# x turned by VectorE in 32x32 blocks instead of by TensorE, in a two-layer decoder trunk on one core

## The chip, the core and the metric

The kernel runs on one core of a Trainium2 chip. The metric is the device time of one execution in microseconds. The kernel before takes 2053.56 us, the median of three runs (2053.30 to 2054.64). One more execution was taken with the hardware profiler; the traces quoted below are of that one.

The engines are named as in the profile: PE is TensorE (PEld its weight loads), DVE VectorE, ACT ScalarE, POOL GpSimd, SP the engine that issues nearly all DMAs. A line such as L155 is a line of the kernel before unless it is said to be of the changed one.

## The reference, cut to what matters

```python
x = x + concat([main, mo]) @ w_out[l]        # once for each of the two layers
# layer 0:
h = rmsnorm(x, g_mix[0])                      # x * rsqrt(mean(x*x) + EPS) * g
z = h @ w_in_a[0]                             # D = 2048 -> 3584 columns
main = spatial_gating(z[..., :G_W], z[..., G_W:2 * G_W], g_v, w_sp, b_sp)
mo = memory_attention(z[..., 2 * G_W:], mem, g_mem[0], w_mem_kv[0])
# after each mixer a gated ConvFFN; layer 1 uses multi-head latent attention
```

The input x has 256 positions and 2048 features, `mem` 256 tokens of 2048 features, all float32. Both layers' keys and values of `mem` depend on no x: `rmsnorm(mem, g_mem[l]) @ w_mem_kv[l]` (2048 to 1024 columns each).

## The kernel before, in words

All matrix products are done in pieces that TensorE takes at its fast rate: each float32 operand is split into a rounded part (hi) and the rest (lo), and three products, hi·hi, hi·lo and lo·hi, are summed. A **chunk** is one 512 KB load of weights into a tile `raw` (four buffers), split by ScalarE into `whi` (four buffers) and by VectorE into `wlo` (five), and used by 24 matmuls of 256 columns (`gemm_fm`, L152, L153, L155) or 12 of 512 columns (`gemm_tm`, L184 to L186). SP issues the load of a chunk as soon as the `raw` buffer that is due comes free, so loads, splits and products run as a pipeline, some chunks ahead of PE.

Activations are kept feature-major: `self.x` (tile `xT`) holds x transposed, 16 blocks of 128 features by 256 positions, and `self.xhl` (tile `xhl`) its halves, multiplied with the gain `g_mix` by `split_gain` (L245 on ScalarE, L246 on VectorE). The root of the mean square is applied later, to the products.

The function `start` does four stages of eight chunks each: keys of `mem` for layer 0 (`first_keys`, in a hand-written order), its values (`gemm_tm`), keys for layer 1 (`gemm_fm`) and its values (`gemm_tm`). A table `hooks` hangs extra work behind chunk n of a stage. From there a scheduler orders the instructions on each engine by its own estimate, within the order in which they were written; `keep_in_program_order` and `manual_schedule` fix some of it. In the kernel before, the hooks bring x in like this:

- `token_load` (L391) loads a quarter of x in rows of 2 KB into the token-major tile `xtok`, in the chunks 0 to 3 of the second stage.
- `token_transpose` (L395) turns two feature blocks with four 128x128 transposes each on PE (L400) into PSUM; `put_x` (L452) splits them from PSUM and copies them into `xT` with ScalarE (L455).
- `token_squares` (L406) sums the squares of x per token on ScalarE; `token_rstd` makes the root `rt` (128x2, one token per partition), and `spread` (L420) makes from it, with two PE matmuls against a diagonal tile, `rb` (root along the free axis on all partitions).
- `conv_consts` (L329) loads four rows of constants `craw` of each ffn and turns them with four PE transposes (L337).

`layer_a` follows: three groups of eight chunks by `gemm_tm` whose evictions apply a Gelu scaled by `rt` (L775), then the rest by `gemm_fm`, whose evictions use `rb`. Its hooks load the spatial weights into the tile `wsp` (four DMAs of 128-byte pieces, L761), which takes the memory of `memhl` and so must wait until PE is done with `start`; VectorE turns them in 32x32 blocks (L766) and multiplies them with a mask (L767). They also load `positions` and, with small instructions on VectorE, make the rotary angles (`rope_angles`, with one PE transpose, L352). At the end of the program the function `turn` in `run` does the opposite of the change for layer 1: it turns `xT` in 32x32 blocks (L1114) and writes them with DMAs of 128-byte pieces (L1118).

Of the kernel before, what the change touches and what calls it, by code (L numbers as in the profile page):

```python
# [8 lines left out]
F32 = mybir.dt.float32  # L9
# [3 lines left out]
AF = mybir.ActivationFunctionType  # L13
ALU = mybir.AluOpType
AX = mybir.AxisListType

P = 128
D = 2048
S = 256
NB = D // P  # L20
# [49 lines left out]
class Kernel:  # L70
# [171 lines left out]

    def split_gain(self, hl, x, g):
        nc = self.nc
        nc.scalar.activation(hl[:, :S], x, AF.Copy, scale=g)  # L245
        nc.vector.scalar_tensor_tensor(hl[:, S:], x, g, hl[:, :S].bitcast(F32), ALU.mult, ALU.subtract)  # L246


    def rstd(self, out, sums, n, pool, tag):
# [79 lines left out]
    def conv_consts(self, l):  # L329
        nc, t = self.nc, self.t  # L330
        nf = 2 * FB
        acc = self.psum()
        for j in range(4):
            cr = self.tmp(self.gp, [nf, P], "craw", 4)
            src = t["conv_w"][l, j] if j < 3 else t["conv_b"][l]
            nc.sync.dma_start(out=cr, in_=src.rearrange("(k p) -> k p", p=P))
            nc.tensor.transpose(acc[:, j * nf : (j + 1) * nf], cr, self.ident[:nf, :nf])  # L337
        nc.vector.tensor_copy(self.cT[:, l], acc[:, : 4 * nf].rearrange("p (j k) -> p j k", j=4))

# [48 lines left out]
        nc.vector.tensor_copy(self.sinT, acc[:, S:])  # L388


    def token_load(self, src, tok, k0, k1):  # L391
        c = slice(k0 * P, k1 * P)
        self.nc.sync.dma_start(out=tok[:, :, c], in_=src.rearrange("(a p) c -> p a c", p=P)[:, :, c])

    def token_transpose(self, tok, k0, k1, put):  # L395
        for k in range(k0, k1, 2):
# [23 lines left out]
    def spread(self, out, r):  # L420
        nc = self.nc
        acc = self.psum()
        for tb in range(2):
            dg = self.tmp(self.cp, [P, P], "diag", 1)
            nc.vector.tensor_scalar(dg, self.ident, r[:, tb : tb + 1], None, ALU.mult)
            nc.tensor.matmul(acc[:, tb * P : (tb + 1) * P], self.ones, dg, start=True, stop=True)
        nc.scalar.activation(out, acc[:, :S], AF.Copy)


    def start(self):  # L430
        nc, t, tc = self.nc, self.t, self.tc
# [4 lines left out]
        self.mv = [pool.tile([P, 2, MW], F32, name=self.uid("mv")) for pool in (self.mk, self.cp)]  # L436
        self.rt = self.cp.tile([P, 2], F32, name="rt0")
        self.rb = self.tmp(self.cp, [P, S], "rbc", 2)
        with tc.tile_pool(name="st", bufs=1) as st:
            self.gp = st  # L440
            mtok = st.tile([P, 2, D], F32, name="mtok")
            xtok = st.tile([P, 2, D], F32, name="xtok")
            mrt = st.tile([P, 2], F32, name="mrt")
            mrb = st.tile([P, S], F32, name="mrb")

# [3 lines left out]
                nc.scalar.activation(hi, a, AF.Copy)  # L449
                nc.vector.tensor_tensor(mhl[:, k : k + 2, S:], a, hi.bitcast(F32), ALU.subtract)  # L450

            def put_x(k, acc):  # L452
                for i in range(2):
                    self.split_gain(self.xhl[k + i], acc[:, i * S : (i + 1) * S], self.gain("g_mix", k + i))
                nc.scalar.activation(self.x[:, k : k + 2, :], acc.rearrange("p (k s) -> p k s", k=2), AF.Copy)  # L455

            mload = lambda k0, k1: lambda: self.token_load(t["mem"][0], mtok, k0, k1)
            mturn = lambda k0, k1: lambda: self.token_transpose(mtok, k0, k1, put_mem)
            xload = lambda k0, k1: lambda: self.token_load(t["x"][0], xtok, k0, k1)
            xturn = lambda k0, k1: lambda: self.token_transpose(xtok, k0, k1, put_x)  # L460
            mpart = st.tile([P, 2, 4], F32, name="mpart")
            xpart = st.tile([P, 2, 4], F32, name="xpart")
            msq = lambda j: lambda: self.token_squares(mtok, mpart, j, st)
            xsq = lambda j: lambda: self.token_squares(xtok, xpart, j, st)

            def scale_keys():
                self.spread(mrb, mrt)
# [9 lines left out]
            def first_keys(evict):  # L477
# [62 lines left out]
                for b, acc in enumerate(accs):  # L540
# [2 lines left out]
            hooks = [  # L543
                None,
                {
                    0: [lambda: self.gains(("g_mix", "g_ffn", "g_kv")), xload(0, 4), msq(0), msq(1)], 1: [xload(4, 8), msq(2), msq(3)],
                    2: [lambda: self.token_rstd(mpart, st, mrt), xload(8, 12)], 3: [xload(12, 16), xturn(0, 4)], 4: [self.masks],
                    6: [lambda: self.gains(("g_v", "g_kv_lat", "g_q_lat"))],
                },
                {0: [xturn(4, 8)], 1: [scale_keys], 2: [xturn(8, 12)], 4: [xturn(12, 16)], 6: [xsq(0)]},  # L550
                {
                    0: [xsq(1)], 1: [xsq(2)], 2: [xsq(3), lambda: self.conv_consts(0)], 3: [lambda: self.token_rstd(xpart, st, self.rt)],
                    5: [lambda: self.spread(self.rb, self.rt), lambda: self.conv_consts(1)],
                },
            ]
            for l in range(2):
# [12 lines left out]
                m = lambda k: mhl[:, k, :]  # L569
                g = lambda k: self.gain("g_mem", l * NB + k)  # L570
# [9 lines left out]
    def three(self, o, w, x, start, stop):  # L580
        mm, (wh, wl), (xh, xl) = self.nc.tensor.matmul, w, x
        mm(o, wh, xh, start=start, stop=False)  # L582
        mm(o, wh, xl, start=False, stop=False)  # L583
        mm(o, wl, xh, start=False, stop=stop)  # L584
# [149 lines left out]
                g0 += ng  # L734


    def layer_a(self):
        nc, t, tc = self.nc, self.t, self.tc
        w, xhl, rt, rb = t["w_in_a"][0], self.xhl, self.rt, self.rb
        x = lambda k: xhl[k]  # L740
        ks = list(range(NB))
        with ExitStack() as ctx:
            la = ctx.enter_context(tc.tile_pool(name="la", bufs=1))
# [19 lines left out]
            def spatial_turn(g):  # L763
                w4 = wT[:, g : g + 4, :]
                k3 = self.keep.rearrange("p (g s) -> p g s", g=1).to_broadcast([P, 4, P])
                nc.vector.transpose(out=w4, in_=spatial["raw"][:, g : g + 4, :])  # L766
                nc.vector.tensor_tensor(w4, w4, k3, ALU.mult)  # L767

            turns = {2 + i: [lambda i=i: spatial_turn(4 * i)] for i in range(3)}
            zhooks = ({2: [lambda: self.rope_angles(la)], 5: [spatial_load]}, {4: [self.rope_tables]}, turns)  # L770
            for c in range(3):

                def evz(tb, acc):
# [30 lines left out]
            hl = self.ap.tile([P, NB, 512], F32R, tag="big", name=self.uid("mainhl"))  # L804
            p, parts = {}, {}
# [388 lines left out]
```

## Time and profile before

| | |
|---|---|
| median of three runs | 2053.56 us |
| profiled execution | 2053.87 us, of which the span 2052.2 us |
| granted TensorE clock | 0.999 |
| start to about 104.3 us | the four stages of `start` |
| from about 104.3 us | `layer_a` |
| L400 on x | 32 transposes, 32.5 to 72.9 us |
| x loads | four of 512 KB, issued from 22.7 to 30.8 us |

How to read it: times are from the span's start. A row of a timeline gives the start, the time that the group took, engine, line, operation, tiles and count, and in brackets the idle time just before with what ended it. PE's matmuls are pipelined, so the end of one lies beyond the start of the next; the distance between starts is what an instruction costs, its duration is not. A row of the groups ends with busy time, mean ns of one, idle time before them. A row for one line gives durations as min/median/max in ns. A row of stretches gives, after the stretch and its length, the busy time and count of PE, PEld, DVE, ACT and POOL, then the granted clock, the DMA share and GB/s. A row of waits gives the total, the number of times and the longest.

### The profile page before, as it was taken

The numbers are of one execution on the slowest core, as the hardware profiler recorded it, in microseconds if no ns is written. First come the engines' busy times: TensorE is split into PE (matmuls) and PEld (weight loads), VectorE is DVE, ScalarE is ACT, GpSimd is POOL, SyncE is SP. The second block draws the span as 40 slices with busy tenths as digits, with TensorE's granted clock in tenths as the row PEclk, the third lists the DMA queues.
The fourth block names the chain that finished last, engine by engine and source line by source line (L and its number), as shares of the span: only waits on it lengthen the run. The fifth ranks groups of instructions, "written<-read, shape, count | busy, mean of one in ns | idle before, by whom it ended". The sixth has DMA issues, their size and how long they took to land.

```text
span 2052.2 us, 39853 instructions
## 1 busy us (share of the span) xinstructions
PE 2042.1 (100%) x16304; PEld 1975.3 (96%) x16304; DVE 1401.0 (68%) x2120; ACT 1083.3 (53%) x1581; POOL 142.1 (7%) x200
## 2 busy tenths in 40 slices
PE   9999999999999999999999999999999999999998
PEld 8989999999999999999999999999988999889996
DVE  6666766777656767557778786777755667646765
ACT  7754744555434555345545575455543555435554
POOL 0000013100000000000043141400000000000000
PEclk9999999999999999999999999999999999999999
DMA  8576555566556665566555535568655666556654
GB/s 286 188 212 185 165 195 194 188 196 195 195 196 193 192 194 194 195 195 192 198 192 180 183 116 179 184 204 223 208 187 194 197 194 195 191 193 195 197 181 154
DMA packets 228987, 394.66 MB, mean 192 GB/s; under 512 B 36990, under 2 KB 44484, under 8 KB 228676
## 3 DMA queue, kind: packets, MB, share of 16 engines
q1 hardware_dynamic: 228612, 391.58, 59.6%
q8 instruction: 127, 2.08, 0.4%
q10 hardware_dynamic: 192, 0.54, 0.1%
q14 instruction: 56, 0.46, 0.1%
HBM read 387.88 MB, written 2.10 MB: 190 GB/s over the span
## 4 chain that ended last, share of the span: by engine, by line
PE 99%; ACT 0%; DVE 0%; DMA 0%; issue 0%; ACTq 0%
PE ps L152 26%; PE ps L153 26%; PE ps L155 26%; PE ps L185 6%; PE ps L184 6%; PE ps L186 6%; PE ps L507 1%; PE ps L400 0%; PE ps L583 0%; PE ps L584 0%; PE ps L582 0%; PE ps L1003 0%; PE ps L792 0%; PE ps L1031 0%; PE ps L625 0%; DMA graw<-in_g_mem 0%
## 5 line engine op out<-in xcount | busy, mean ns | idle before, releaser
L114 DVE TENSOR_TENSOR wlo<-raw,whi 128x1024 fp32r<-128x1024 f32 x660 | 818.5, 1243 | 521.9 <-ACT whi L113 516.1
L113 ACT ACTIVATE whi<-raw 128x1024 fp32r<-128x1024 f32 x660 | 700.5, 1062 | 851.7 <-PE ps L153 616.9
L152 PE MATMUL ps<-xhl,whi 128*128 128x256 f32 x3264 | 762.7, 277 | 0.0
L153 PE MATMUL ps<-xhl,whi 128*128 128x256 f32 x3264 | 761.1, 276 | 0.0
L152 PEld LDWEIGHTS ps<-xhl,whi 128*128 128x128 f32 x3264 | 612.7, 188 | 0.3
L153 PEld LDWEIGHTS ps<-xhl,whi 128*128 128x128 f32 x3264 | 612.7, 188 | 0.3
L155 PE MATMUL ps<-xhl,wlo 128*128 128x256 f32 x3264 | 436.5, 276 | 0.0
L155 PEld LDWEIGHTS ps<-xhl,wlo 128*128 128x128 f32 x3264 | 400.3, 188 | 0.0
L152 PE MATMUL ps<-h,whi 128*128 128x256 f32 x704 | 163.6, 276 | 0.0
L153 PE MATMUL ps<-h,whi 128*128 128x256 f32 x704 | 163.6, 276 | 0.0
L185 PE MATMUL ps<-wlo,h 128*128 128x512 f32 x354 | 137.2, 388 | 0.0
L184 PE MATMUL ps<-whi,h 128*128 128x512 f32 x354 | 136.8, 388 | 0.0
L186 PE MATMUL ps<-whi,h 128*128 128x512 f32 x354 | 136.8, 388 | 0.0
L153 PEld LDWEIGHTS ps<-h,whi 128*128 128x128 f32 x704 | 131.9, 188 | 0.0
L152 PEld LDWEIGHTS ps<-h,whi 128*128 128x128 f32 x704 | 131.8, 188 | 0.0
L152 PE MATMUL ps<-mainhl,whi 128*128 128x256 f32 x512 | 119.6, 277 | 0.0
L153 PE MATMUL ps<-mainhl,whi 128*128 128x256 f32 x512 | 119.3, 276 | 0.0
L694 ACT ACTIVATE c<-a,cT 128x256 f32<-128x256 f32 x176 | 99.3, 589 | 0.4 <-DVE a L232 0.3
L153 PEld LDWEIGHTS ps<-mainhl,whi 128*128 128x128 f32 x512 | 96.0, 188 | 0.0
L152 PEld LDWEIGHTS ps<-mainhl,whi 128*128 128x128 f32 x512 | 95.9, 188 | 0.0
L155 PE MATMUL ps<-h,wlo 128*128 128x256 f32 x704 | 94.1, 276 | 0.0
L232 DVE TENSOR_TENSOR a<-ps,rbc 128x256 f32<-128x256 f32 x176 | 69.9, 418 | 24.9 <-PE ps L155 24.9
(318 smaller groups left out, 2251.2 us busy)
## 6 DMA issues: line engine op xcount, KB each, us to landing
raw<-in_w_ffn_up SPq DMA_DIRECT2D x352, 512.0 KB, 3.5
raw<-in_w_ffn_down SPq DMA_DIRECT2D x176, 512.0 KB, 4.6
raw<-in_w_out SPq DMA_DIRECT2D x64, 512.0 KB, 4.3
raw<-in_w_in_a SPq DMA_DIRECT2D x56, 512.0 KB, 3.5
raw<-in_w_mem_kv SPq DMA_DIRECT2D x31, 512.0 KB, 4.4
raw<-in_w_in_b SPq DMA_DIRECT2D x16, 512.0 KB, 3.5
raw<-in_w_kv_a SPq DMA_DIRECT2D x9, 512.0 KB, 4.0
raw<-in_w_uq SPq DMA_DIRECT2D x12, 384.0 KB, 3.3
```

The source lines that it names most:

```text
L113: nc.scalar.activation(hi[:, :n], raw[:, :n], AF.Copy)
L114: nc.vector.tensor_tensor(lo[:, :n], raw[:, :n], hi[:, :n].bitcast(F32), ALU.subtract)
L152: mm(acc[:, :S], wh, x[:, :S], start=first, stop=False)
L153: mm(acc[:, :S], wh, x[:, S:], start=False, stop=False)
L155: mm(acc[:, :S], wl, x[:, :S], start=False, stop=last)
L184: mm(acc, xh, wh, start=first, stop=False)
L185: mm(acc, xh, wl, start=False, stop=False)
L186: mm(acc, xl, wh, start=False, stop=last)
L232: self.nc.vector.tensor_tensor(out, acc[:, :S], r, ALU.mult)
L507: nc.tensor.matmul(acc[:, :S], w[:, o : o + P], x, start=k == 0 and n == 0, stop=k == NB - 1 and n == 2)
L694: nc.scalar.activation(c, a, AF.Identity, scale=w(2), bias=w(3))
```

## The change

x is loaded with its positions on partitions 0 to 31 of a quarter: portion m holds positions 32m to 32m + 31, and its four DMAs put feature columns 32q to 32q + 31 of every 128 on partitions 32q to 32q + 31, in pieces of 32 floats (128 bytes). One VectorE transpose of 32x32 blocks per portion then writes 32 columns of all 16 blocks of `xT`. The portions, four DMAs of 64 KB each, are spread over hooks of the second and third stage, the transposes come two or three chunks after the loads. The squares are taken on ScalarE from `xT` (two blocks at a time) and added up by VectorE into `xsum`; the sum over partitions is a PE matmul with `ones` in the new `x_rstd`, called in chunk 4 of `layer_a`'s first group, which replaces `token_squares`, `token_rstd` and `spread` for x. The splits with gain move to the fourth stage and read `xT`. The loads of the conv constants are kept in the written order.

```diff
-    def token_load(self, src, tok, k0, k1):
-        c = slice(k0 * P, k1 * P)
-        self.nc.sync.dma_start(out=tok[:, :, c], in_=src.rearrange("(a p) c -> p a c", p=P)[:, :, c])
+    def block_load(self, src, raw, m):
+        s = src[32 * m : 32 * (m + 1), :].rearrange("i (k q j) -> q i k j", q=4, j=32)
+        for q in range(4):
+            self.tc.keep_in_program_order(self.nc.sync.dma_start(out=raw[32 * q : 32 * (q + 1), m], in_=s[q]))
...
-            nc.sync.dma_start(out=cr, in_=src.rearrange("(k p) -> k p", p=P))
+            self.tc.keep_in_program_order(nc.sync.dma_start(out=cr, in_=src.rearrange("(k p) -> k p", p=P)))
...
-            dg = self.tmp(self.cp, [P, P], "diag", 1)
+            dg = self.tmp(self.cp, [P, P], "diag", 2)
...
-            def put_x(k, acc):
-                for i in range(2):
-                    self.split_gain(self.xhl[k + i], acc[:, i * S : (i + 1) * S], self.gain("g_mix", k + i))
-                nc.scalar.activation(self.x[:, k : k + 2, :], acc.rearrange("p (k s) -> p k s", k=2), AF.Copy)
+            def xturn(m):
+                keep(nc.vector.transpose(out=self.x[:, :, 32 * m : 32 * (m + 1)], in_=xraw[:, m]))
+
+            def xput(k):
+                sq = xsum if k == 0 else self.tmp(st, [P, 512], "junk", 2).rearrange("p (k s) -> p k s", k=2)
+                keep(nc.scalar.activation(sq, self.x[:, k : k + 2, :], AF.Square))
+                if k:
+                    keep(nc.vector.tensor_tensor(xsum, xsum, sq, ALU.add))
+                for j in (k, k + 1):
+                    for ins in self.split_gain(self.xhl[j], self.x[:, j, :], self.gain("g_mix", j)):
+                        keep(ins)
+                if k == NB - 2:
+                    nc.vector.tensor_tensor(self.ssum, xsum[:, 0], xsum[:, 1], ALU.add)
...
                 {
-                    0: [lambda: self.gains(("g_mix", "g_ffn", "g_kv")), xload(0, 4), msq(0), msq(1)], 1: [xload(4, 8), msq(2), msq(3)],
-                    2: [lambda: self.token_rstd(mpart, st, mrt), xload(8, 12)], 3: [xload(12, 16), xturn(0, 4)], 4: [self.masks],
-                    6: [lambda: self.gains(("g_v", "g_kv_lat", "g_q_lat"))],
+                    0: [lambda: self.gains(("g_mix", "g_ffn", "g_kv")), msq(0), msq(1)], 1: [msq(2), msq(3)],
+                    2: [lambda: self.token_rstd(mpart, st, mrt), xload(0)], 4: [self.masks, xload(1)], 5: [xt(0)],
+                    6: [lambda: self.gains(("g_v", "g_kv_lat", "g_q_lat")), xload(2)], 7: [scale_keys, xt(1)],
                 },
-                {0: [xturn(4, 8)], 1: [scale_keys], 2: [xturn(8, 12)], 4: [xturn(12, 16)], 6: [xsq(0)]},
                 {
-                    0: [xsq(1)], 1: [xsq(2)], 2: [xsq(3), lambda: self.conv_consts(0)], 3: [lambda: self.token_rstd(xpart, st, self.rt)],
-                    5: [lambda: self.spread(self.rb, self.rt), lambda: self.conv_consts(1)],
+                    0: [xload(3)], 1: [xload(4), xt(2)], 2: [xt(3)], 3: [xload(5), xt(4)], 4: [xload(6)], 5: [xload(7), xt(5)],
+                    6: [xt(6)], 7: [xt(7)],
+                },
+                {
+                    0: [xp(0)], 1: [xp(2)], 2: [lambda: self.conv_consts(0), xp(4)], 3: [xp(6)], 4: [xp(8)],
+                    5: [lambda: self.conv_consts(1), xp(10)], 6: [xp(12)], 7: [xp(14)],
                 },
...
+    def x_rstd(self):
+        self.rstd_bc(self.rb, self.ssum, D)
+        acc = self.psum()
+        for tb in range(2):
+            self.nc.tensor.matmul(acc[:, tb : tb + 1], self.ssum[:, tb * P : (tb + 1) * P], self.ones[:, :1], start=True, stop=True)
+        self.rstd(self.rt, acc[:, :2], D, self.cp, "rt")
...
-            zhooks = ({2: [lambda: self.rope_angles(la)], 5: [spatial_load]}, {4: [self.rope_tables]}, turns)
+            zhooks = ({2: [lambda: self.rope_angles(la)], 4: [self.x_rstd], 5: [spatial_load]}, {4: [self.rope_tables]}, turns)
```

**The order on the engines.** Three places. First PE in the third stage, between the stage's first chunk and its second, in the kernel before (`ps` are accumulators, the numbers tell tiles of one name apart):

```order
L155 MATMUL ps_687<-memhl_82,wlo_691 128x256 x2
L155 MATMUL ps_688<-memhl_82,wlo_691 128x256 x2
L400 MATMUL ps_721<-ident,xtok 128x128 x4
L400 MATMUL ps_731<-ident,xtok 128x128 x4
L152 MATMUL ps_685<-memhl_82,whi_742 128x256
```

The changed kernel has no L400 with `xtok` anywhere; its x work on PE stands in chunk 5 of `layer_a`:

```order
L352 MATMUL ps_1293<-ident,pos_f 128x2
L265 MATMUL ps_1401<-ssum_89,ones 128x256
L755 MATMUL ps_1412<-ones,ssum_89 128x1 x2
```

So eight transposes here, and 32 in all, have gone, and three matmuls have come. Second SP's loads in the second stage, before:

```order
L317 DMA graw_469<-in_g_kv 16x128
L393 DMA xtok<-in_x 128x2x512
L103 DMA raw_485<-in_w_mem_kv 128x2x512
L393 DMA xtok<-in_x 128x2x512
L103 DMA raw_514<-in_w_mem_kv 128x2x512
L393 DMA xtok<-in_x 128x2x512
```

and now:

```order
L317 DMA graw_470<-in_g_kv 16x128
L103 DMA raw_485<-in_w_mem_kv 128x2x512
L103 DMA raw_513<-in_w_mem_kv 128x2x512
L394 DMA xraw<-in_x 32x16x32 x4
L103 DMA raw_548<-in_w_mem_kv 128x2x512
L103 DMA raw_568<-in_w_mem_kv 128x2x512
L394 DMA xraw<-in_x 32x16x32 x4
```

The x loads stand two weight loads later and in groups of four; the last group stands ahead of the twelfth weight load counted from `raw_548`. Third VectorE at the start of `layer_a`, before (`wlo_1426` is chunk 5 of its first group, `wlo_1450` chunk 6):

```order
L114 TENSOR_TENSOR wlo_1408<-raw_1406,whi_1407 128x1024
L350 CAST pos_f<-pos_i 2x128
L114 TENSOR_TENSOR wlo_1426<-raw_1424,whi_1425 128x1024
L766 STREAM_TRANSPOSE slots_1255<-wsp_1443 128x512 x3
L114 TENSOR_TENSOR wlo_1450<-raw_1448,whi_1449 128x1024
```

and now:

```order
L114 TENSOR_TENSOR wlo_1385<-raw_1383,whi_1384 128x1024
L788 STREAM_TRANSPOSE slots_1232<-wsp_1443 128x512 x3
L789 TENSOR_TENSOR slots_1232<-slots_1232,keep 128x512
L114 TENSOR_TENSOR wlo_1426<-raw_1424,whi_1425 128x1024
L789 TENSOR_TENSOR slots_1232<-slots_1232,keep 128x512
L350 CAST pos_f<-pos_i 2x128
```

The transposes of `wsp` and a mask product have moved ahead of chunk 5's `wlo`, and the cast behind it. On SP the four `wsp` loads are now issued together, ahead of chunk 6's load and of `in_b_sp`, which stood between them before.

More of the change, by code (lines that the diff above doesn't have):

```diff
@@ L244, in split_gain @@
         nc = self.nc
-        nc.scalar.activation(hl[:, :S], x, AF.Copy, scale=g)
-        nc.vector.scalar_tensor_tensor(hl[:, S:], x, g, hl[:, :S].bitcast(F32), ALU.mult, ALU.subtract)
+        hi = nc.scalar.activation(hl[:, :S], x, AF.Copy, scale=g)
+        return hi, nc.vector.scalar_tensor_tensor(hl[:, S:], x, g, hl[:, :S].bitcast(F32), ALU.mult, ALU.subtract)
     def rstd(self, out, sums, n, pool, tag):
@@ L438, in start @@
         self.rb = self.tmp(self.cp, [P, S], "rbc", 2)
+        self.ssum = self.tmp(self.cp, [P, S], "ssum", 2)
         with tc.tile_pool(name="st", bufs=1) as st:
@@ L441, in start @@
             mtok = st.tile([P, 2, D], F32, name="mtok")
-            xtok = st.tile([P, 2, D], F32, name="xtok")
+            xraw = st.tile([P, 8, NB, 32], F32, name="xraw")
+            xsum = st.tile([P, 2, S], F32, name="xsum")
             mrt = st.tile([P, 2], F32, name="mrt")
@@ L450, in put_mem @@
                 nc.vector.tensor_tensor(mhl[:, k : k + 2, S:], a, hi.bitcast(F32), ALU.subtract)
-            def put_x(k, acc):
-                for i in range(2):
-                    self.split_gain(self.xhl[k + i], acc[:, i * S : (i + 1) * S], self.gain("g_mix", k + i))
-                nc.scalar.activation(self.x[:, k : k + 2, :], acc.rearrange("p (k s) -> p k s", k=2), AF.Copy)
[L457 to L460, printed above, removed]
+            keep = tc.keep_in_program_order
+            def xturn(m):
[10 more added lines that the diff above has]
+                    nc.vector.tensor_tensor(self.ssum, xsum[:, 0], xsum[:, 1], ALU.add)
+            xload = lambda m: lambda: self.block_load(t["x"][0], xraw, m)
+            xt = lambda m: lambda: xturn(m)
+            xp = lambda k: lambda: xput(k)
             mpart = st.tile([P, 2, 4], F32, name="mpart")
-            xpart = st.tile([P, 2, 4], F32, name="xpart")
             msq = lambda j: lambda: self.token_squares(mtok, mpart, j, st)
-            xsq = lambda j: lambda: self.token_squares(xtok, xpart, j, st)
             def scale_keys():
```

## The prediction

> **What bounds the kernel now.** I read the page's busy times first, then its chain, then TensorE's own waits.
>
> ```profile
> PE 2042.1 (100%) x16304; PEld 1975.3 (96%) x16304; DVE 1401.0 (68%) x2120; ACT 1083.3 (53%) x1581; POOL 142.1 (7%) x200
> ...
> PE 99%; ACT 0%; DVE 0%; DMA 0%; issue 0%; ACTq 0%
> ```
>
> The chain that ends last is TensorE from end to end. The waits view of PE has three rows in all:
>
> ```profile
> PE ps L474 <- DVE ones L283: 1.1, 1, 1.1
> PE ps L583 <- DVE pT L241: 0.4, 1, 0.4
> PE ps L325 <- DMA graw<-in_g_mem: 0.4, 1, 0.4
> ```
>
> 1.9 us of waiting in a span of 2052.2, and none of it where the change works (20 to 130 us). So time is won only by instructions taken from PE, and lost only if VectorE, ScalarE or the weight loads fall so far behind that PE begins to wait. The unit below is the chunk: one 512 KB weight load, 24 matmuls of 256 columns.
>
> **The change part by part.** *PE loses the transposes of x* (the first place shown in the part on the change). Rows of PE's timeline in the third stage, where eight transposes stand between two chunks:
>
> ```profile
> 57.98 1.07 PE L155 MATMUL ps<-memhl,wlo 128*128 128x256 f32 x8
> 58.89 1.04 PE L400 MATMUL ps<-ident,xtok 128*128 128x128 f32 x8
> 61.60 1.07 PE L155 MATMUL ps<-memhl,wlo 128*128 128x256 f32 x8
> ...
> 68.55 1.07 PE L155 MATMUL ps<-memhl,wlo 128*128 128x256 f32 x8
> 71.27 1.08 PE L155 MATMUL ps<-memhl,wlo 128*128 128x256 f32 x8
> ```
>
> From one chunk's L155 to the next is 71.27 - 68.55 = 2.72 us bare and 61.60 - 57.98 = 3.62 us with eight transposes: 0.90 us for eight, the switch to and from them included. There are 32 on x: **-3.60 us**.
>
> *PE loses `spread` of x's root* (two matmuls with `diag`):
>
> ```profile
> 97.98 0.39 PE L426 MATMUL ps<-diag,ones 128*128 128x128 f32 x2
> 98.20 0.47 PE L337 MATMUL ps<-ident,craw 88*128 88x88 f32 x4
> ...
> 102.90 0.39 PE L426 MATMUL ps<-diag,ones 128*128 128x128 f32 x2
> 103.04 0.47 PE L185 MATMUL ps<-wlo,memhl 128*128 128x512 f32 x1
> 103.35 0.40 PE L186 MATMUL ps<-whi,memhl 128*128 128x512 f32 x1
> 103.59 0.40 PE L184 MATMUL ps<-whi,memhl 128*128 128x512 f32 x1
> ```
>
> 98.20 - 97.98 = 0.22, and 103.35 - 102.90 = 0.45 less one ordinary step (103.59 - 103.35 = 0.24) = 0.21: **-0.43 us**.
>
> *PE gains `x_rstd`*: a matmul of `ones` with the 256-column sum, as L265 does in the ffn, and two with one column.
>
> ```profile
> 367.70 1.07 PE L155 MATMUL ps<-xhl,wlo 128*128 128x256 f32 x8
> 368.61 0.59 PE L265 MATMUL ps<-ssum,ones 128*128 128x256 f32 x2
> 370.88 1.07 PE L155 MATMUL ps<-xhl,wlo 128*128 128x256 f32 x8
> ```
>
> 370.88 - 367.70 = 3.18, less 2.72: **+0.46 us**. An fp32 matmul shows as two passes (x2), so the one-column ones are four passes. No row has such a shape: between nothing and four passes at the 0.11 us a 128-column fp32 pass takes above (0.90 / 8), 0.44. I take **+0.40**, near the upper end, since the 128 x 128 weights are loaded all the same. Sum on PE: -3.60 - 0.43 + 0.46 + 0.40 = **-3.2 us** (-3.6 to -3.1 with the bounds).
>
> *VectorE gains* eight block transposes of 128x512, seven additions of 128x512, one of 128x256, and the root on 256 columns. The nearest rows:
>
> ```profile
> 116.22 1.90 DVE L766 STREAM_TRANSPOSE slots<-wsp 128x512 f32<-128x512 f32 x3 [3.96 <-DMA wsp<-in_w_sp]
> 118.04 1.18 DVE L114 TENSOR_TENSOR wlo<-raw,whi 128x1024 fp32r<-128x1024 f32 x1
> 119.21 1.89 DVE L767 TENSOR_TENSOR slots<-slots,keep 128x512 f32<-128x512 f32 x3
> ...
> L246 DVE SCALAR_TENSOR_TENSOR xhl<-xT,gT,xhl x32: 830/894/961, 294.7 to 1329.9; 128x256 fp32r<-128x256 f32 x32
> L246 DVE SCALAR_TENSOR_TENSOR xhl<-ps,gT,xhl x16: 470/476/484, 41.1 to 79.0; 128x256 fp32r<-128x256 f32 x16
> L246 DVE SCALAR_TENSOR_TENSOR qhl<-ql,gT,qhl x4: 474/474/474, 1151.3 to 1153.2; 128x256 fp32r<-128x256 f32 x4
> ```
>
> A transpose is 1.90 / 3 = 0.63 us, an addition 0.63: 8 x 0.63 + 7 x 0.63 + 0.4 = 9.9 us over some 75 us. The 16 splits with gain read `xT` from SBUF instead of PSUM; that is 0.47 (the `qhl` row) to 0.89 us (the `xhl<-xT` row), so 0 to 6.7 us more; I take 0, because the long rows stand where GpSimd squares the same `xT`, and it does not here. ScalarE drops eight copies and trades squares for squares. Of that, nothing is on the chain as long as VectorE's lead lasts:
>
> ```profile
> 54.44 1.42 DVE L119 SCALAR_TENSOR_TENSOR wlo<-raw,gT,whi 128x512 fp32r<-128x512 f32 x2 [1.30 <-ACT whi L118]
> ...
> 64.65 1.12 PE L155 MATMUL ps<-memhl,wlo 128*128 128x256 f32 x8
> ```
>
> That chunk's `wlo` is ready at 55.86 and used at 64.65: 8.8 us ahead. VectorE is 65 to 75% busy here (rows below), so 9.9 us spread over 27 chunks, 0.37 of each 2.72, fits: cost 0.
>
> *The loads.* x comes in 16384 pieces of 128 bytes instead of 2 KB rows. The trace has one stretch like it, where `turn` writes x back through 16 transfers of 1024 such pieces; beside it the stretch before, weights alone, and the stretches that x will now fall in:
>
> ```profile
> 1340.00:1384.00 44.00, 44.00 (x390) 44.00 (x390) 33.21 (x53) 24.95 (x33) 0.00 (x0) 1.00 0.62 192
> 1384.00:1418.00 34.00, 34.00 (x302) 34.00 (x301) 22.13 (x29) 14.62 (x19) 0.00 (x0) 1.00 0.95 206
> ...
> 42.00:56.00 14.00, 14.00 (x63) 11.33 (x62) 10.36 (x23) 11.76 (x21) 0.00 (x0) 1.00 0.64 218
> 56.00:72.00 16.00, 16.00 (x141) 15.96 (x140) 10.76 (x19) 13.35 (x27) 3.29 (x4) 1.00 0.53 174
> ...
> xt<-xs SPq DMA_DIRECT2D x16, 128.0 KB, 6.2
> ...
> DVE wlo L114 <- ACT whi L113: 12.2, 8, 4.7
> ```
>
> (last columns: clock, DMA share, GB/s). Weights cost 16 x 0.62 / 0.192 = 52 engine-us per MB. From 1384 to 1418, 7.0 MB moved in 0.95 x 16 x 34 = 517 engine-us; 4.9 MB of weights take 253, the 2.1 MB of pieces 264: 16 ns a piece, or 16.5 us of all sixteen engines, where 2 KB rows would take 6.8. The eight portions stand among twelve weight loads (SP's order, in the part on the change), 12 x 2.72 = 32 us: at a share of 0.6 the weights take 19.2 of these, with the pieces 35.7, so the feed may fall 3.7 us behind; the lead is 8.8. In the stretch quoted VectorE did wait, up to 4.7 us for one chunk (last row), and PE was busy 34.00 of 34.00. Cost 0. Each block transpose stands behind the `wlo` of a chunk whose load was issued after its own portion, so it adds no wait of its own.
>
> The Trainium skill, "DMA: Bandwidth & Descriptors", Specifications, speaks against this part: below 512 B a transfer misses line rate, by read-modify-write. The trace agrees in kind (16.5 us against 6.8 for the same bytes). By the rule alone the first rival below would be the likelier and its time the answer; by the rows the price is paid off PE's chain, and the sum stays.
>
> *The start of layer A* is where cover is thinnest. VectorE's transposes of `wsp`, which wait for the four `w_sp` loads, now stand ahead of chunk 5's `wlo`, not chunk 6's, and the cast for PE's L352 stands behind them.
>
> ```profile
> 104.28 0.40 PE L184 MATMUL ps<-whi,xhl 128*128 128x512 f32 x1
> ...
> 104.47 1.12 SPq L761 DMA_DIRECT2D wsp<-in_w_sp  x2
> ...
> 107.60 0.39 SPq L755 DMA_DIRECT2D slots<-in_b_sp  x1
> 108.04 1.60 SPq L761 DMA_DIRECT2D wsp<-in_w_sp  x2
> ...
> SPq L761 <- PE ps L186: 0.2, 1, 0.2
> ```
>
> The loads wait for PE to leave `memhl` (last row), that is for layer A's begin, T (104.28). They landed at 116.22, T + 11.9, with `in_b_sp` (0.79 MB, 0.79 x 52 / 16 = 2.6 us) among them; now it is issued after them, so about T + 9.4. Then three transposes 1.9, one mask product 0.63, `wlo` 1.2: ready T + 13.1; PE reaches it at 5 x 2.72 + 0.46 = T + 14.1. Another product and the cast end at T + 13.9, and PE's L352 stands at T + 14.5. So 0.6 us to spare, cost 0; at worst they land as late as before, and PE loses 2.5 - 0.6 = 1.9 us. Behind that, `x_rstd` adds about 4 us on VectorE (the 256-column reciprocal alone 1.75, next row) while PE goes through chunks 7 to 12. From T + 13.1 to chunk 9's `wlo` I add 10.1 us: T + 23.2, wanted at T + 25.8.
>
> ```profile
> L257 DVE RECIPROCAL rbr<-rbr 128x256 f32<-128x256 f32 x1 | 1.8, 1754 | 0.5 <-ACT rbr L256 0.5
> ```
>
> *The constants' loads* leave the first 20 us, where no chunk waited for them: 0.
>
> The profiled execution took 2053.87 us, 1.67 outside its span; 2053.87 - 3.2 = 2050.7. The median of the runs shown is 2053.56, 0.3 lower, so the forecast is **2050.4 us**, 0.16% faster.
>
> **The rivals.** *The feed starves* (slower than before). If a piece costs much more than 16 ns when it comes from HBM, the weights behind it on the same queue are late, `raw` is empty, and the lead is used up. For: the strained row above, and SP's issue of four piece transfers. Against: PE held there. It decides from (32 + 8.8 - 19.2) us x 16 / 16384 = 21 ns a piece; at twice the 16 ns, 19.2 + 33 - 40.8 = 11.4 us are lost: 2061.8. The rule above points the same way.
>
> *`w_sp` lands late*: worked out above, 2052.3; it decides from T + 10.0.
>
> *PE gets more than the pitch says.* If a transpose really holds PE for its whole duration, 32 times that is gained:
>
> ```profile
> L400 PE MATMUL ps<-ident,xtok x32: 270/272/274, 32.6 to 72.9; 128*128 128x128 f32 x32
> ```
>
> 32 x 0.272 = 8.7 instead of 3.6: 2045.3. Against it stand the 0.90 us for eight. The Trainium skill, "TensorE: Matmul & The Clock Gate", Part 4: PE-mode transpose, puts a transpose inside a kernel at about 275 ns; this trace's duration agrees, its spacing does not.
>
> *Nothing changes*: some other wait takes the 3.2 us, most likely `rt` so late that the Gelu holds ScalarE. 2053.5.
>
> **How the numbers follow.** Forecast 0.60 (2049.8 to 2051.2 by the bounds); `w_sp` late 0.12 (to 2053); feed starves 0.18, mostly over 2057.7; more from PE 0.05; nothing 0.05. About 0.2%, 4.1 us, is what a measurement of this kernel tells from no change, so -3.2 counts as the same: faster 0.11 (0.05, and 0.06 of the forecast, should the spacing of neighbouring chunks tighten by 0.9 us in all), same 0.70, slower 0.19. The range, 2049.2 to 2055.5, takes in the forecast, late `w_sp`, no change and the mildest starving.
>
> **What would show it.** Right: PE's waits view has no new row between 20 and 130 us, chunks are 2.72 us apart throughout the third stage, and layer A begins 3.6 to 4.2 us earlier. Feed: rows of PE waiting for VectorE or ScalarE in L152 to L186 before 100 us, or `whi` waiting for `raw` by several us. `w_sp`: PE waiting at chunk 5 of layer A. What would make the forecast wrong otherwise: block transposes far over 0.63 us, or one-column matmuls over 0.1 us a pass.

## The result, and the profile after

The changed kernel takes **2049.85 us** (median of 22 runs, 2049.50 to 2051.64), the kernel before 2053.43 in as many. The ratio is 0.9983, 95% interval 0.9977 to 0.9989: 3.5 us faster, between 2.3 and 4.7 (3.6 by the medians). The forecast was 2050.4, that is 3.2 us less. Both are under the 4.1 us from which the prediction counts a change, so this is its "same", to which it gave 0.70. The profiled execution took 2050.37 us with a span of 2048.6, against 2053.87 and 2052.2.

The page's busy times and chain, and then all of PE's waits, of the changed kernel:

```profile
PE 2038.7 (100%) x16274; PEld 1972.0 (96%) x16274; DVE 1411.5 (69%) x2138; ACT 1079.5 (53%) x1565; POOL 142.5 (7%) x200
...
PE 99%; ACT 0%; DVE 0%; DMA 0%; issue 0%; ACTq 0%
```

```profile
PE ps L485 <- DVE ones L283: 1.1, 1, 1.1
PE ps L597 <- DVE pT L241: 0.4, 1, 0.4
PE ps L325 <- DMA graw<-in_g_mem: 0.3, 1, 0.3
```

PE is still the wall and its waits are the same three. VectorE has 10.5 us more to do, ScalarE 3.8 less. So the gain has to lie in PE's own instructions, and where it lies can be read from the first matmul of each stage. PE's timeline before, at the begin of the second, third and fourth stage of `start` and of the part of layer A that follows its three `gemm_tm` groups (layer A's own begin, 104.28, was shown in the prediction):

```profile
32.02 0.40 PE L184 MATMUL ps<-whi,memhl 128*128 128x512 f32 x1
...
56.15 0.28 PE L152 MATMUL ps<-memhl,whi 128*128 128x256 f32 x1
...
81.25 0.40 PE L184 MATMUL ps<-whi,memhl 128*128 128x512 f32 x1
...
170.47 0.28 PE L152 MATMUL ps<-xhl,whi 128*128 128x256 f32 x1
```

and now, with layer A's begin:

```profile
31.93 0.40 PE L184 MATMUL ps<-whi,memhl 128*128 128x512 f32 x1
...
55.51 0.37 PE L152 MATMUL ps<-memhl,whi 128*128 128x256 f32 x1
...
77.38 0.40 PE L184 MATMUL ps<-whi,memhl 128*128 128x512 f32 x1
...
99.94 0.39 PE L184 MATMUL ps<-whi,xhl 128*128 128x512 f32 x1
...
166.97 0.28 PE L152 MATMUL ps<-xhl,whi 128*128 128x256 f32 x1
```

| stretch of PE | before | after | difference |
|---|---|---|---|
| span's start to the third stage | 56.15 | 55.51 | -0.64 |
| third stage (24 of the 32 transposes stood here) | 25.10 | 21.87 | -3.23 |
| fourth stage (`spread` stood here) | 23.03 | 22.56 | -0.47 |
| layer A's three groups (`x_rstd` stands here now) | 66.19 | 67.03 | +0.84 |
| from there to the span's end | 1881.73 | 1881.63 | -0.10 |
| sum | 2052.2 | 2048.6 | -3.6 |

Of the first -0.64, the second stage makes -0.55 (24.13 us before, 23.58 now). The other 0.09, like the 0.10 at the end, stands where PE's work hasn't changed; without both, the stages that the change touches give -3.41. Layer A begins 4.34 us earlier, a little more than the 3.6 to 4.2 that the prediction named as its sign.

In the third stage each chunk now follows the last at the bare distance: 62.87 - 60.15 = 2.72 us.

```profile
60.15 0.28 PE L155 MATMUL ps<-memhl,wlo 128*128 128x256 f32 x1
...
62.87 0.39 PE L155 MATMUL ps<-memhl,wlo 128*128 128x256 f32 x2
```

The price of `x_rstd` stands in chunk 5 of layer A's first group. From PE's timeline:

```profile
114.76 0.22 PE L352 MATMUL ps<-ident,pos_f 2*128 2x2 f32 x1
114.91 0.70 PE L265 MATMUL ps<-ssum,ones 128*128 128x256 f32 x2
115.45 0.50 PE L755 MATMUL ps<-ones,ssum 128*128 128x1 f32 x4
115.81 0.48 PE L185 MATMUL ps<-wlo,xhl 128*128 128x512 f32 x1
```

The four one-column passes last from 115.45 to 115.81. On VectorE, the block transposes, and a pair of splits that read `xT` from SBUF:

```profile
L458 DVE STREAM_TRANSPOSE xT<-xraw x8: 703/704/706, 42.5 to 71.8; 128x512 f32<-128x512 f32 x8
```

```profile
73.76 0.87 DVE L246 SCALAR_TENSOR_TENSOR xhl<-xT,gT,xhl 128x256 fp32r<-128x256 f32 x2
```

So far the sum holds. What the experiments had to settle is whether the covers are as thick as the prediction made them: it costed 16384 small pieces, 9.9 us of VectorE and a late `w_sp` at nothing.

### The profile page after: what moved, and what is told of

It is laid out like the page before. It is cut to its first block, busy times and chain, and to the rows that moved or that the text cites. A ratio compares the mean times of both kernels' runs of the same rounds, so it can differ in the third digit from the quotient of the medians.

```text
span 2048.6 us, 39833 instructions
## 1 busy us (share of the span) xinstructions
PE 2038.7 (100%) x16274; PEld 1972.0 (96%) x16274; DVE 1411.5 (69%) x2138; ACT 1079.5 (53%) x1565; POOL 142.5 (7%) x200
## 4 chain that ended last, share of the span: by engine, by line
PE 99%; ACT 0%; DVE 0%; DMA 0%; issue 0%; ACTq 0%
PE ps L152 26%; PE ps L153 26%; PE ps L155 26%; PE ps L184 6%; PE ps L185 6%; PE ps L186 6%; PE ps L518 1%; PE ps L597 0%; PE ps L598 0%; PE ps L596 0%; PE ps L1025 0%; PE ps L814 0%; PE ps L401 0%; PE ps L1053 0%; PE ps L639 0%; DMA graw<-in_g_mem 0%
```

## The experiments

All are made from the changed kernel. Times are to be read against 2049.85, stages against the table above. The start of the program varies by itself: among kernels that are the same up to there, the third stage begins between 54.55 and 56.53 us in their profiles. Lengths of stages don't share this: the second stage takes 23.58 to 23.68 us in all of these.

**What a transpose costs PE.** Two kernels with 24 idle transposes:

```diff
+            def one():
+                acc = self.psum()
+                nc.tensor.transpose(acc[:, :P], mtok[:, 0, :P], self.ident)
...
+            for stage in hooks[1:]:
+                for n in range(8):
+                    stage.setdefault(n, []).append(one)
```

> The changed kernel, with 24 idle PE transposes of 128x128 put back (their result is read by nobody), one behind each chunk of the second, third and fourth stage, 18 of them with no other fp32 work beside them. Theory (a transpose costs PE its distance to the next start, 0.11 us, wherever it stands): 24 x 0.11 = +2.6 us, about 2052.5, and chunks of the third stage 2.72 + 0.11 = 2.83 us apart. Rival (a transpose alone between other matmuls holds PE for its duration of 0.27 us, and is cheap only in a run of eight): +6.5 us, about 2056.4, chunks 2.99 us apart.

Measured: 2053.45 us. The third stage takes 22.83 us, 0.96 more for eight (0.12 each); the fourth 23.54, 0.98 more. PE's timeline there:

```profile
62.11 1.07 PE L155 MATMUL ps<-memhl,wlo 128*128 128x256 f32 x8
63.02 0.27 PE L473 MATMUL ps<-ident,mtok 128*128 128x128 f32 x1
64.96 1.07 PE L155 MATMUL ps<-memhl,wlo 128*128 128x256 f32 x8
```

The lone transpose shows 0.27 us and adds 64.96 - 62.11 - 2.72 = 0.13. The second stage takes 0.94 more as well, so the three stages add 2.9. The median is 3.6 us up; the 0.7 left over lies in none of these and was not explained (in its profile the second stage began late, at 32.82). Even so it is far from the rival's +6.5.

```diff
+            def eight():
+                acc = self.psum()
+                for i in range(8):
+                    nc.tensor.transpose(acc[:, i % 4 * P : (i % 4 + 1) * P], mtok[:, 0, :P], self.ident)
...
+            for n in (1, 3, 5):
+                hooks[2][n].append(eight)
```

> The changed kernel, with the same 24 idle transposes in three runs of eight, behind chunks 1, 3 and 5 of the third stage. Theory: 3 x 0.90 = +2.7 us, about 2052.5, the same as one at a time, and the chunks with a run 3.62 us apart. Rival (272 ns each): +6.5 us.

Measured: 2052.56 us, third stage 24.57, so +2.70 for 24. Both say 0.11 to 0.13 us each; the next matmul doesn't wait out the duration of 0.27. The rival that PE gets 0.272 us back per transpose is out.

**The constants' loads.**

```diff
-            self.tc.keep_in_program_order(nc.sync.dma_start(out=cr, in_=src.rearrange("(k p) -> k p", p=P)))
+            nc.sync.dma_start(out=cr, in_=src.rearrange("(k p) -> k p", p=P))
```

> The changed kernel, with the loads of the conv constants left to the scheduler again, which puts them among the first five weight loads; nothing else differs on any engine. Theory (no chunk waits for them there): 0, layer A's first matmul stays at 99.9 us. Rival (a part of the gain comes from the emptier start): slower by up to 0.4 us, all of it before the second stage begins.

Measured: 2050.26 us (2049.48 to 2051.20); the third stage begins at 55.26, layer A at 99.68, all stages as in the table. The median is 0.4 us up, which the rival allows too, but no stage is longer and layer A begins no later. So no part of the gain is seen to come from here, and 0.4 us can't be told from the start's own variation.

**The pieces left out.**

```diff
-                keep(nc.vector.transpose(out=self.x[:, :, 32 * m : 32 * (m + 1)], in_=xraw[:, m]))
+                keep(nc.vector.transpose(out=self.x[:, :, 32 * m : 32 * (m + 1)], in_=xraw[:, 0]))
...
-            xload = lambda m: lambda: self.block_load(t["x"][0], xraw, m)
+            xload = lambda m: lambda: self.block_load(t["x"][0], xraw, 0) if m == 0 else None
```

> The changed kernel, with only the first of the eight portions of x loaded, and all eight block transposes reading that one: seven eighths of the 128-byte pieces are left out. Theory (the pieces cost lead, not time): 0 (within 0.3 us), layer A's first matmul at 99.9 us, but the lead of VectorE's halves over PE in the third stage, 3.8 to 6.3 us in the changed kernel, grows to 7 or more. Rival (the pieces hold PE up somewhere): faster by 0.5 us or more.

Measured: 2049.95 us, stages 21.86, 22.56 and 67.04: no time, as expected. The lead did grow. PE's first need of a chunk is the first half of its `whi`, which ScalarE has ready 0.73 us after it starts. Chunk 22, the last but one of the third stage, on ScalarE and PE, first in the changed kernel:

```profile
67.83 4.01 ACT L118 ACTIVATE whi<-raw,gT 128x512 fp32r<-128x512 f32 x6 [1.95 <-DMA raw<-in_w_mem_kv]
```

```profile
71.94 0.28 PE L152 MATMUL ps<-memhl,whi 128*128 128x256 f32 x1
```

and without the pieces:

```profile
62.28 1.34 ACT L118 ACTIVATE whi<-raw,gT 128x512 fp32r<-128x512 f32 x2 [1.38 <-PE ps L153]
```

```profile
71.14 0.28 PE L152 MATMUL ps<-memhl,whi 128*128 128x256 f32 x1
```

71.94 - 68.56 = **3.4 us** of lead against 71.14 - 63.01 = 8.1; the bracket tells the rest, since ScalarE waits for the load in the one and for PE in the other. Seven eighths of the pieces cost 4.7 us of lead, and no time.

The DMA engines have little left either. Their share (the last column but one) in the changed kernel is 1.00 and 0.84 where it was 0.64 and 0.53 before:

```profile
42.00:56.00 14.00, 14.00 (x66) 11.44 (x66) 9.35 (x21) 8.27 (x16) 0.00 (x0) 1.00 1.00 244
56.00:72.00 16.00, 16.00 (x143) 16.00 (x143) 11.82 (x17) 9.98 (x17) 3.63 (x4) 1.00 0.84 245
```

**More pieces.** How much more could the feed have borne? Portions are loaded once more, into `mtok`, which is free by then: behind the last one, the last two, the last four, and behind each of the last four two. The edit is that of the first; the second and third have `m >= 6` and `m >= 4` in it, the fourth loads two portions for each `m > 3`.

```diff
+            xdup = mtok.rearrange("p a (b k j) -> p (a b) k j", b=4, j=32)
+            dup = lambda m: self.block_load(t["x"][0], xdup, m) if m >= 7 else None
-            xload = lambda m: lambda: self.block_load(t["x"][0], xraw, m)
+            xload = lambda m: lambda: (self.block_load(t["x"][0], xraw, m), dup(m))
```

> The changed kernel, with one portion more (2048 pieces, 4 DMAs) behind the last, into a tile that nobody reads. In the changed kernel SP issues without a pause from 42 to 63 us, 0.64 us for each of these DMAs, and the smallest lead of VectorE's halves in the third stage is 3.75 us. Theory (SP's issue time is taken from the lead): 4 x 0.64 = 2.6 us of lead lost, about 1.2 left, time unchanged, 2049.9. Rival (time of the DMA engines): 1.8 us of lead lost, time unchanged as well.

> The changed kernel, with two portions more, one behind each of the last two. Theory (SP's issue time): 8 x 0.64 = 5.1 us against 3.75 of lead, so the third stage, 21.87 us in the changed kernel, takes 1.4 us more, and some more where the granted clock falls after PE has stood: 2051.2 to 2053. Rival (engine time): 3.6 us against 3.75, time unchanged.

> The changed kernel, with four portions more, one behind each of the last four. Theory (SP's issue time): 16 x 0.64 = 10.3 us against 3.75, so 6.5 us and some clock: 2056 to 2059. Rival (engine time): 4 x 1.8 = 7.2 less 3.75 less some free time of the engines, +2: 2052.

> The changed kernel, with 16384 more pieces of 128 bytes: behind each of the portions 4 to 7 two more portions are loaded into a tile that nobody reads. Theory of the prediction (what counts is the time of the 16 DMA engines): at about 14 ns a piece 14.3 us more; the engines have about 9% of 20 us free there, and the halves lead PE by at least 3.8 us: 14.3 - 1.8 - 3.8 = +8.7 us, about 2058.5, and PE waits for halves in the third stage. Rival (SP, which needs 0.63 us for the issue of each of the 32 DMAs, 20.2 us in all, is the limit): 20.2 - 3.8 less what SP has free, 12 us or more, 2062 or later. Third: the feed has more room than either, 0 to +3.

| portions more | time | over 2049.85 |
|---|---|---|
| 1 | 2052.92 | +3.1 |
| 2 | 2055.39 | +5.5 |
| 4 | 2060.14 | +10.3 |
| 8 | 2072.70 | +22.9 |

One portion, an eighth more pieces, already costs time; both theories said it would not. (Two of its executions took 2049.9 and 2050.0, eight 2052.0 to 2054.7.) With two and four portions the theory with SP's issue time is nearer, but too low by 2.4 and 1.1 us at its upper end, and engine time is too low by 5.5 and 8. PE's timeline around chunk 22 of the run with one portion more, and its clock in two stretches behind (the column before the last two):

```profile
73.95 0.39 PE L152 MATMUL ps<-memhl,whi 128*128 128x256 f32 x1 [2.35 <-ACT whi L118]
...
76.94 1.91 PE L155 MATMUL ps<-memhl,wlo 128*128 128x256 f32 x8
78.64 0.40 PE L152 MATMUL ps<-memhl,whi 128*128 128x256 f32 x1
```

```profile
74.00:76.00 2.00, 1.89 (x12) 1.68 (x13) 2.00 (x4) 1.98 (x4) 0.00 (x0) 0.87 0.90 346
76.00:78.00 2.00, 2.00 (x11) 2.00 (x10) 2.00 (x4) 1.27 (x3) 0.00 (x0) 0.50 0.70 208
```

PE stands 2.35 us, and 1.5 us after it has begun again it is granted half its clock for some 3 us, so that the chunk takes 78.64 - 73.95 = 4.69 us instead of 2.72. The third stage is 4.61 us longer in this execution (2054.48 us), nearly twice the wait.

Why did 3.4 us of lead not carry one portion of 2.6? SP's row of one load ahead of the last two portions, in the changed kernel, and in this one with the added portion:

```profile
54.95 1.68 SPq L103 DMA_DIRECT2D raw<-in_w_mem_kv  x1
```

```profile
54.60 3.71 SPq L103 DMA_DIRECT2D raw<-in_w_mem_kv  x1
...
64.93 2.92 SPq L394 DMA_DIRECT2D mtok<-in_x  x4
```

The added DMAs take SP 2.9 us, and this load, ahead of them, 2.0 more than in the other execution. Chunk 22's load is the first of the five that follow the last portion, in the changed kernel and then here:

```profile
63.01 7.38 SPq L103 DMA_DIRECT2D raw<-in_w_mem_kv  x5
```

```profile
67.95 7.80 SPq L103 DMA_DIRECT2D raw<-in_w_mem_kv  x5
```

It is issued 4.9 us later, and ScalarE begins on it 4.8 us behind its issue in the changed kernel and 5.2 here (67.83 and 73.18). So the load is late because SP issues it late, and hardly because it takes longer. Why the load at 54.60 held SP for 3.71 us isn't shown. I take it that such pushes come and go between executions, which agrees with the two that lost nothing; that they do in the changed kernel as well wasn't shown.

With eight portions more, a row of SP's timeline and what its eight DMAs took, two stretches of the core, and PE's largest row of waits:

```profile
60.61 7.09 SPq L394 DMA_DIRECT2D mtok<-in_x  x8
```

```profile
L394 SPq DMA_DIRECT2D mtok<-in_x x8: 581/626/2383, 60.6 to 67.1; - x8
...
DMA to landing us min/median/max: 2.4/2.5/2.7
```

```profile
56.00:72.00 16.00, 11.39 (x94) 10.66 (x92) 4.07 (x6) 2.91 (x5) 2.83 (x4) 1.00 0.82 167
72.00:88.00 16.00, 10.09 (x48) 9.50 (x48) 3.46 (x5) 2.67 (x4) 0.00 (x0) 0.68 0.76 126
```

```profile
PE ps L152 <- ACT whi L118: 14.2, 4, 5.9
```

The DMA share is 0.82 and 0.76, so the sixteen engines are not full; SP issues without a pause from 47 to 88 us (its 48 DMAs of pieces take 35.9 us of these, 0.75 each), and PE waits 14.2 us in four waits. The eight DMAs of the row land 2.4 to 2.7 us after their issue, x's in the changed kernel after 3.2 to 5.2, so these don't stand long at the engines. That bears out the rival with SP's issue time as the limit, which said 12 us or more; engine time alone (+8.7) is wrong. The Trainium skill, "Perfetto Trace Analysis", What "DMA-bound" means, names this case: an issuing sequencer that is solid with DMA slices is the bound, and what it does in them is make descriptors. The trace agrees that SP issues without a pause; what SP does meanwhile no run here shows.

The same bytes in larger pieces:

```diff
+            xrow = lambda c: tc.keep_in_program_order(
+                nc.sync.dma_start(out=mtok[:, :, c], in_=t["x"][0].rearrange("(a p) c -> p a c", p=P)[:, :, c]))
-            xload = lambda m: lambda: self.block_load(t["x"][0], xraw, m)
+            xload = lambda m: lambda: (self.block_load(t["x"][0], xraw, m), m > 3 and xrow(slice(512 * (m - 4), 512 * (m - 3))))
```

> The changed kernel, with the same 2 MB more at the same four places, in four loads of 512 KB with pieces of 2 KB, into a tile that nobody reads. Theory (engine time): 1024 pieces at about 90 ns are 5.8 us of the 16 engines, 5.8 - 1.8 - 3.8 = 0, so the time stays at 2049.9 (to +1); the distance to the run with 128-byte pieces is what the size of the pieces costs. Rival (bytes count, not pieces): the same loss as with the small pieces.

Measured: 2057.93 us, +8.1. So 2 MB cost 22.9 - 8.1 = 14.8 us more in 128-byte pieces and 32 DMAs than in 2 KB pieces and four; these runs don't separate the size of the pieces from the number of DMAs. The theory's "nothing" for the rows was wrong, and so was the rival's "the same loss". Here the engines are full, in the stretch in which PE falls behind:

```profile
56.00:72.00 16.00, 13.85 (x118) 13.25 (x117) 6.16 (x9) 6.66 (x11) 3.19 (x4) 1.00 1.04 247
72.00:88.00 16.00, 14.86 (x91) 13.65 (x92) 11.83 (x22) 10.05 (x19) 0.00 (x0) 0.89 0.88 285
```

And the eight portions issued by GpSimd, with the engine as a further argument of `block_load` (the edit is against the kernel with eight portions more):

```diff
-            dup = lambda m: [self.block_load(t["x"][0], xdup, 2 * m - 8 + i) for i in range(2 * (m > 3))]
+            dup = lambda m: [self.block_load(t["x"][0], xdup, 2 * m - 8 + i, nc.gpsimd) for i in range(2 * (m > 3))]
```

> The changed kernel, with the 16384 further pieces of the run that cost 22.9 us, but issued by GpSimd from its own queue (behind its work on the keys, so from about 59 us on) instead of by SP. Theory (that run was slow because SP's queue was full of issues, so that the weights behind them came late): SP is as free as in the changed kernel, and what is left is the engines' time, 14.3 us less about 6 free from 56 to 84 us less 3.75 of lead: +4 to +8. Rival (the pieces themselves hold the DMA engines, whoever issues them): +20 or more again.

Measured: 2065.42 us, +15.6, between the two. PE's largest wait is now another one, for the conv constants in the fourth stage:

```profile
PE ps L337 <- DMA craw<-in_conv_w: 6.7, 1, 6.7
```

Theory (+4 to +8) and rival (+20) both miss. How much of the 22.9 is SP's and how much the engines' stays open. Issued this way the pieces come later and hit other loads, and the page's row for GpSimd's queue counts the 2.1 MB as 1024 packets, not as 16384 pieces, so more than the issuing engine has changed:

```profile
q0 software_dynamic: 1024, 2.10, 0.5%
```

**More work on VectorE.**

```diff
-                keep(nc.vector.transpose(out=self.x[:, :, 32 * m : 32 * (m + 1)], in_=xraw[:, m]))
+                for _ in range(3):
+                    keep(nc.vector.transpose(out=self.x[:, :, 32 * m : 32 * (m + 1)], in_=xraw[:, m]))
```

> The changed kernel, with each block transpose done three times: 16 more on VectorE, 16 x 0.70 = 11.2 us between 42 and 72 us, where VectorE is busy 21.2 of 30 us. Theory (VectorE is covered by its idle time, 8.8 us, and by its lead of 3.8 us or more): 0 to +1 us, with the lead at the start of the fourth stage down to about 1.5 us. Rival (VectorE is what sets the pace here as soon as it gets more work): most of the 11.2 us show, over 2055.

Measured: 2051.74 us (2049.49 to 2054.62). Third and fourth stage stay at 21.87 and 22.56, but layer A's groups take 68.27, 1.24 more. SP, VectorE and PE there (layer A begins at 101.03):

```profile
103.36 5.71 SPq L784 DMA_DIRECT2D wsp<-in_w_sp  x4
```

```profile
112.90 1.90 DVE L789 STREAM_TRANSPOSE slots<-wsp 128x512 f32<-128x512 f32 x3 [3.50 <-DMA wsp<-in_w_sp]
114.72 1.19 DVE L114 TENSOR_TENSOR wlo<-raw,whi 128x1024 fp32r<-128x1024 f32 x1
```

```profile
115.96 0.50 PE L185 MATMUL ps<-wlo,xhl 128*128 128x512 f32 x1 [0.94 <-DVE wlo L114]
```

The median is 1.9 us up, more than the theory's 0 to +1 and less than the rival's.

VectorE's delay is not seen where it arises. It comes out 30 us later. VectorE ends its work for x (`ssum`) 1.6 us after layer A's begin in the changed kernel and 6.8 us after it here. SP's waits in the 21 us around layer A's begin, in the changed kernel and then here:

```profile
SPq L103 <- DVE wlo L119: 8.4, 4, 3.6
SPq L103 <- DVE wlo L114: 4.3, 3, 2.7
SPq L783 <- PE ps L186: 2.0, 1, 2.0
```

```profile
SPq L103 <- DVE wlo L119: 10.5, 5, 4.4
SPq L103 <- DVE wlo L114: 4.6, 2, 2.5
```

In the changed kernel SP is early and waits 2.0 us for PE's last product of `start` before the `w_sp` loads. Here its weight loads ahead of them wait 2.4 us longer for VectorE to free `raw`, and it gets to `w_sp` only 2.3 us after layer A's begin; `w_sp` lands at T + 11.9, and PE waits for chunk 5's `wlo`. That is the rival of a late `w_sp`, with its landing time exactly; it cost 1.24 us where I had said 1.9.

**A version without the one-column matmuls.**

```diff
-        acc = self.psum()
-        for tb in range(2):
-            self.nc.tensor.matmul(acc[:, tb : tb + 1], self.ssum[:, tb * P : (tb + 1) * P], self.ones[:, :1], start=True, stop=True)
-        self.rstd(self.rt, acc[:, :2], D, self.cp, "rt")
+        for tb in range(2):
+            dg = self.tmp(self.cp, [P, P], "diag", 2)
+            self.nc.vector.tensor_tensor(dg, self.rb[:, tb * P : (tb + 1) * P], self.ident, ALU.mult)
+            self.nc.vector.tensor_reduce(self.rt[:, tb : tb + 1], dg, AX.X, ALU.add)
```

> The changed kernel, with the root per token taken from the root along the free axis by VectorE (a product with the identity and a sum along the free axis, twice), and so without the two one-column matmuls. Theory (an fp32 pass with one column costs PE 0.11 us like one with 128): -0.44 us, 2049.4, to be seen as a shorter way from layer A's first matmul to its fourth group, 67.03 us in the changed kernel, 66.6 here. Rival: the root comes about 1 us later, so that the Gelu of the first group holds ScalarE and PE waits for a half: 0 to +1.

Measured: 2049.68 us (0.9982 of before, 0.9973 to 0.9991). Layer A's groups take 66.61, 0.42 less; the times can't tell it from the changed kernel. (Its profile, of its slowest execution, takes 1.0 us more from there to the end, where the edit changes nothing on PE; 0.6 of it is a wait at 1418.7.) A pass with one column costs 0.11 us, like one with 128.

## Why the prediction was right, step by step

- **PE loses 32 transposes, 3.60.** Right: 24 of them (24 x 0.1125 = 2.70) and four passes of `spread` for `mem`, which stood in the third stage and now stand just ahead of it (0.45), make 3.15 of the 3.23 there. The other eight, less these four passes, lie in the -0.64 before it, with the varying start.
- **`spread` 0.43.** Measured 0.47. **`x_rstd` 0.86.** Measured 0.84; the one-column passes were rightly put near the upper bound (0.42 of 0.44). The sum of -3.2 thus came from the right terms, where the stages give -3.41; the measured 3.5 and the profile's 3.6 differ from it by less than the start varies.
- **VectorE, cost 0.** Right in time. The block transposes took 0.70 alone; 0.63 was the price in a run of three. The additions took 0.68, so transposes and additions come to 10.9 us for 9.9. A pair of splits took 0.87, the end that I had chosen. (The 10.5 that the page has more is another sum: it has the root's work in it as well, and lacks what fell away.)
- **The loads, cost 0.** Right, but with a thinner cover than stated, and this is the step with wrong sizes. The lead was put at 8.8 us, and the loss at 3.7, so 5.1 would have been left; measured are 8.1, 4.7 and 3.4. Two things were left out. The lead was taken at `wlo`, though PE first needs `whi`. And the loss was worked out from the engines' time alone, while SP spends 2.57 us on the four DMAs of a portion. The price of a piece was not too low: in the trace the pieces took about 14 ns each, not 16, which would leave 1.4 us of loss by the prediction's own sum. That the rest of the 4.7 is SP's is the likeliest reading, not a shown one.
- **The starved feed decides from 21 ns a piece, and doubled costs 11.4.** Too mild on both counts: an eighth more pieces made most executions slower, and doubling them cost 22.9. SP's issue comes on top, which the sum left out, and PE ran at a lower clock behind its waits (0.68 from 72 to 88 us). The chance of 0.18 rested on a margin of 31% in the price of the pieces; an eighth more of them was past it. That this didn't happen in the changed kernel is thus partly luck: the cover held by 3.4 us, not by the 5.1 that the prediction had.
- **`w_sp`, 0.6 us to spare.** It landed at T + 8.5 (108.44 - 99.94), a little better than T + 9.4, and `wlo` of chunk 5 was ready 1.95 us ahead. The order of the loads kept it; a VectorE that is later undoes it.
- **The constants' loads, 0.** Right as far as it can be told: 0.4 us by the medians, less than the start varies.

## What to carry to other kernels

Where one engine is busy from end to end, what a change saves is the distance between starts of the instructions that leave it, not their durations. What the other engines take on costs nothing as long as the lead lasts, and the lead is to be measured at the first operand that the wall needs, for the worst chunk, with the issuing engine's time counted beside that of the DMA engines. A gain like this one is safe only if the cover is tested too: here an eighth more pieces took 3.1 of the 3.6 us back.

## What the runs showed of the hardware

- After a wait of 2.35 us PE was granted half its clock for about 3 us (0.50 from 76 to 78 us), so the wait cost twice its length. The Trainium skill, "TensorE: Matmul & The Clock Gate", HAM oscillation — how this bites in real kernels, asks for no gap above some 3.4 us; here a shorter one was enough, and the measurement decides.
- SP takes 0.63 us (median) to issue a DMA of 512 pieces of 128 bytes. Single ones take longer, up to 2.38 among the eight of the row above, which makes 0.89 each there (7.09 / 8); what SP waits for in these no run here shows.
- 2 MB issued by GpSimd count as 1024 packets on a queue of their own; issued by SP, the trace has them as pieces of 128 bytes.
- A 128x128 fp32 transpose shows 0.27 us and adds 0.11 to 0.13 us to PE's stream of matmuls.
